# Other start addresses for split weights and matmul operands in a two-block transformer kernel

## The chip, the cores and the metric

The kernel runs on one core of one Trainium2 chip. The metric is the device time of one execution in microseconds (us). Before the change it is 894.39 us, the median of three runs (894.35 to 894.55).

## What is computed

Two transformer blocks over 256 tokens of width 1024, in float32. Nearly all the work is products of the activations with large weight matrices:

```python
# block one
proj = rms_norm(x) @ w_in                  # then block attention and gated linear attention
x = x + concat([y_moba, y_gla]) @ w_out
h = causal_dwconv(rms_norm(x) @ w_ffn_up)  # 1024 -> 2 * 2816
x = rms_norm(x + (silu(h_gate) * h_val) @ w_ffn_down)
# block two
x = x + 0.5 * g1 * swiglu(modulate(rmsnorm(x)), ffn1_w_in, ffn1_w_out)
z = modulate(rmsnorm(x)) @ w_in            # then latent attention and chunk attention
x = x + g2 * ((sigmoid(gate_a) * (o_a @ w_branch_a) + sigmoid(gate_b) * (o_b @ w_branch_b)) @ w_out)
x = rmsnorm(x + 0.5 * g3 * swiglu(modulate(rmsnorm(x)), ffn2_w_in, ffn2_w_out))
```

## The kernel before

Activations lie feature by token: 128 features in the partitions, 256 tokens (`S`) side by side, and the 1024 features of a row block as `KD = 8` tiles. A weight matrix is read as tiles of 128x128, and each is the stationary operand of a matmul with 256 (or 258) columns of activations moving past it.

To keep float32 precision at the fast matmul rate, each number is split into a high and a low half (`F32R`). A product then takes three matmuls: weight high x activation high, weight high x activation low, weight low x activation high. Where the two halves of an activation lie side by side in one tile (`Operand.beside`), the first two are one matmul of 512 columns, and the product is a pair: one of 512 columns and one of 256 (`lin_b`).

Weights come in chunks of up to 1024 columns, eight 128x128 tiles. `Stream` loads a chunk by a DMA on SyncE's queue into `wraw` (5 buffers), ScalarE copies it into `whi`, VectorE subtracts to get `wlo` (4 buffers each, used in turn). The order of all instructions on each engine is fixed when the program is built: a planner with a model of costs (`Clock`) decides when the side work of attention, norms and splits is slipped between the matmuls. That model knows nothing of addresses.

The stages, in order, with what the stream of weights meets in each:

| stage | moving operand | steps |
|---|---|---|
| attention input of block one (`mix1`) | `xhi`, `xlo`, 256 columns | 336 of 256 columns; 96 with the weights moving, 512 columns |
| `out1` | `yh`, `yl` | 192 of 256 columns |
| `up1` | `nh`, `nl` | 960 of 256 columns, after 64 plain float32 ones |
| `down1` | `hh` (high and low side by side) | 176 pairs of 512 and 256 columns |
| `ff1up` | raw `xhi`, `xlo` (258 columns), then `nh` | 240 of 258 columns, then 816 of 256 |
| `ff1down` | `hh` | 176 pairs |
| `mix2`, merge, `out2` | `xhi`/`xlo`, `nh`/`nl`, `qlh`/`qll` (latents), `oah`, `obh`, `mh` | 936 of 256 columns on `nh`, `oa`, `ob` and `mh`; others |
| `ff2up` | raw `xhi`, `xlo` (258 columns), then `nh` (side by side) | 240 of 258 columns, then 272 pairs |
| `ff2down` | `hh` | 176 pairs |

Each tile has an address in SBUF, the same in all 128 partitions. A tile starts where the one before it in its pool ended. In the built program all buffers of `whi` and `wlo` are 4096 bytes long and all start at 32 bytes modulo 512, and a 128-column slice is 512 bytes, so every weight tile starts at 32 modulo 512. So do `yh`, `yl`, `nh`, `nl`, `hh`, `oah`, `obh`, `mh` and `ml`, whose rows are 1024 or 2048 bytes. Others lie elsewhere: `xhi` at 192 and `xlo` at 256 modulo 512, and `qlh` and `qll` at 224. In the raw stages a row of `xhi` and `xlo` is 258 columns, 1032 bytes, so each step of the contraction starts 8 bytes further on.

The tiles that the change touches: `hi` and `lo` in `Stream.prep` (lines 240 and 241), `yo` (977), `ho` and `no` of the first feed-forward (1239 and 1240) and of `swiglu` (1390 and 1391), with `Operand.beside`. What follows are the functions that the diff touches and what calls them.

Of the kernel before, what the change touches and what calls it, by code (L numbers as in the profile page):

```python
# [11 lines left out]
F32R = mybir.dt.float32r  # L12
# [6 lines left out]
P = 128  # L19
D = 1024  # L20
S = 256
KD = D // P
FF = 2816
NF = FF // P
CH = 1024
# [69 lines left out]
def plan():  # L95
# [6 lines left out]
    def group(entries, width=CH, whole=False):  # L102
        first = len(chunks)
        cur, w = [], 0
        for e in entries:
            ew = sum(b - a for a, b in e[2])
            if w + ew > width:
                chunks.append(cur)
                cur, w = [], 0
            cur.append(e)  # L110
            w += ew
        if cur:
            chunks.append(cur)
        if whole:
            uncut.update(range(first, len(chunks)))

    def lin(name, c0, nk=KD, whole=False):
        group(tiles_t(name, [(c0, c0 + P)], nk), whole=whole)
# [25 lines left out]
    def ffn(up, down):  # L144
        for n in range(NF):
            lin(up, P * n, whole=up == "w_ffn_up" and n < RAW_PAIRS[up])
            lin(up, FF + P * n, whole=up == "w_ffn_up" and n < RAW_PAIRS[up])
        group([(down, k, [(P * n, P * n + P)]) for n in range(8) for k in range(NF)])
# [28 lines left out]


BESIDE = {"ffn2_w_in_2"}
RAW_PAIRS = {'w_ffn_up': 2, 'ffn1_w_in_2': 5, 'ffn2_w_in_2': 5}  # L180
PLAN, UNCUT = plan()
CW = [sum(b - a for e in c for a, b in e[2]) for c in PLAN]
# [26 lines left out]
class Stream:  # L209
# [20 lines left out]
    def prep(self, upto):  # L230
        while self.n_prep <= min(upto, len(PLAN) - 1):
            c = self.n_prep
            w = CW[c]
            self.load(c)
            raw = self.raw.pop(c)
            self.n_prep += 1
            if c in UNCUT:
                self.ready[c] = (raw, raw)
                continue
            hi = self.pool.tile([P, CH], F32R, name="whi", bufs=SPLIT_BUFS)  # L240
            lo = self.pool.tile([P, CH], F32R, name="wlo", bufs=SPLIT_BUFS)
            self.act.activation(hi[:, :w], raw[:, :w], AF.Copy)
            self.ready[c] = (hi, lo)
            self.owed[c] = (raw, self.clock.t["act"])
# [46 lines left out]
class Operand:  # L291
# [7 lines left out]
    @classmethod  # L299
    def beside(cls, t, n):  # L300

        o = cls(t[:, :, 0:S], t[:, :, S:2 * S], n)
        o.both = t
        return o


class Clock:
# [212 lines left out]
def mark(clock, gen, flag):  # L520
    yield from gen
    flag.append(clock.last)
# [18 lines left out]
SPLIT_BUFS = 4  # L541
# [3 lines left out]
def block_kernel(ctx: ExitStack, tc: tile.TileContext, xin, wst, adaw, cin, vec, cst_a, cst_b, cst_l, wgu, pos,  # L545
# [72 lines left out]
    def spl(op, k, src, scale=None, w=S):  # L618

        hi, lo = op.h[:, k, :w], op.l[:, k, :w]  # L620
        if scale is None:
            A.activation(hi, src, AF.Copy)
        else:
            A.activation(hi, src, AF.Copy, scale=scale)
        yield
        if scale is None:
            V.tensor_tensor(lo, src, hi.bitcast(F32), OP.subtract)
        else:
            V.scalar_tensor_tensor(lo, src, scale, hi.bitcast(F32), op0=OP.mult, op1=OP.subtract)
        op.done[k] = True  # L630
# [250 lines left out]
    ypool = yctx.enter_context(tc.tile_pool(name="y1", bufs=1))  # L881
# [16 lines left out]
    for h in range(4):  # L898
        k = slice(2 * h, 2 * h + 2)
# [74 lines left out]
    gq = one.tile([P, 2, S], F32, name="gq", tag="gqt")  # L974
    gk = one.tile([P, 2, S], F32, name="gk", tag="gkt")

    yo = Operand(ypool.tile([P, KD, S], F32R, name="yh"), ypool.tile([P, KD, S], F32R, name="yl"), KD)
    am = {}

    STAGES = [(hp, tt) for hp in range(2) for tt in range(2)]  # L980
# [197 lines left out]
    def table(name, *kinds):  # L1178

        while any(s[2] in kinds for s in side.live):  # L1180
            yield
        A.preload_act_table_set(name)
# [53 lines left out]
    fctx = ExitStack()  # L1236
    hpool = fctx.enter_context(tc.tile_pool(name="hid1", bufs=1))
    fp = fctx.enter_context(tc.tile_pool(name="ffn1p", bufs=2))
    ho = Operand.beside(hpool.tile([P, NF, 2 * S], F32R, name="hh"), NF)
    no = Operand(hpool.tile([P, KD, S], F32R, name="nh"), hpool.tile([P, KD, S], F32R, name="nl"), KD)  # L1240
    r_row = const.tile([P, S], F32, name="r_row")
    ring = [hpool.tile([P, S + 2], F32, name=f"u{i}") for i in range(4)]
    for u in ring:
# [45 lines left out]
    for n in range(NF):  # L1289
        op = xo if n < RAW_PAIRS["w_ffn_up"] else no  # L1290
        side.room("gate", 2)
# [3 lines left out]
        cu = fp.tile([P, S], F32, name="cu", bufs=3)  # L1295
        if n < RAW_PAIRS["w_ffn_up"]:
            pads = [ring[cnt % 4], ring[(cnt + 1) % 4]]
# [38 lines left out]
    def late(n):  # L1336
        while state["ga"] is None:
            yield
        yield from spl(xo, n, x[:, n, :], state["ga"][:, n:n + 1])
# [47 lines left out]

    def swiglu(name, up, down, norm, xo, r_row, r_norm, a, sh, emit, mid=None, late=None):
        with tc.tile_pool(name=name, bufs=1) as hpool, tc.tile_pool(name=name + "p", bufs=2) as fp:
            ho = Operand.beside(hpool.tile([P, NF, 2 * S], F32R, name="hh"), NF)  # L1390
            no = Operand.beside(hpool.tile([P, KD, 2 * S], F32R, name="nh"), KD)

            def chain():
                yield from norm()
                yield
                yield from normalised(no, x, a, r_norm, sh)

            def gate_raw(g, b, ps):
                while not state["norm"]:
                    yield  # L1400
                V.tensor_tensor(g, ps[:, :S], r_row, OP.mult)
                V.tensor_copy(b, ps[:, S:S + 1])
                yield
                A.activation(g, g, AF.Silu, bias=b)

            def whole(t, ps):

                A.activation(t, ps[:, S:], AF.Copy)
                yield
                V.tensor_tensor(t, ps[:, :S], t, OP.add)  # L1410

            def gate_norm(g, ps):
                if beside:
                    yield from whole(g, ps)
                    yield
                    A.activation(g, g, AF.Silu)
                else:
                    A.activation(g, ps[:, :S], AF.Silu)
                yield

            def value(n, u, g, ps, is_raw, flag):
                if is_raw:
                    while not state["norm"]:
                        yield
                    V.tensor_tensor(u, ps[:, :S], r_row, OP.mult)
                    yield
                    while not flag:
                        yield
                    V.scalar_tensor_tensor(u, u, ps[:, S:S + 1], g, op0=OP.add, op1=OP.mult)
                else:  # L1430
                    if beside:
                        yield from whole(u, ps)
                    while not flag:
                        yield
                    V.tensor_tensor(u, u if beside else ps[:, :S], g, OP.mult)
                yield
                yield from spl(ho, n, u)

            beside = up in BESIDE

            def product():
                return lin_b(up, no, KD) if beside else lin_t(up, no, S)

            by.phase(name + "up")
            state["norm"] = False
            side.add(chain(), "chain", True)
            if late is not None:
                side.add(late(), "late")
            for n in range(NF):
                side.room("gate", 2)  # L1450
                side.room("pair", 2)
                g = fp.tile([P, S], F32, name="g", bufs=3)
                u = fp.tile([P, S], F32, name="u", bufs=3)
                fl = []
                if n < RAW_PAIRS[up]:
                    b = fp.tile([P, 1], F32, name="b", bufs=3)
                    side.run(mark(clock, gate_raw(g, b, lin_t(up, xo, S + 2)), fl), "gate")
                    side.run(value(n, u, g, lin_t(up, xo, S + 2), True, fl), "pair")
                else:
                    side.run(mark(clock, gate_norm(g, product()), fl), "gate")  # L1460
                    side.run(value(n, u, g, product(), False, fl), "pair")
                if mid is not None and n == 12:
                    side.add(mid())
            side.add(table(LNEXP, "gate", "pair"))
            side.room("late", 1)
            by.phase(name + "down")
            for n in range(KD):
                ps = lin_b(down, ho, NF)
                side.room("after", 2)
                side.run(emit(n, ps), "after")  # L1470
            side.drain()
# [69 lines left out]
    ypool = yctx.enter_context(tc.tile_pool(name="y2", bufs=1))  # L1541
    oa = Operand(ypool.tile([P, 4, S], F32R, name="oah"), ypool.tile([P, 4, S], F32R, name="oal"), 4)
    ob = Operand(ypool.tile([P, 4, S], F32R, name="obh"), ypool.tile([P, 4, S], F32R, name="obl"), 4)
    no = Operand(ypool.tile([P, KD, S], F32R, name="nh"), ypool.tile([P, KD, S], F32R, name="nl"), KD)
# [3 lines left out]
    w = "w_in_2"  # L1548
# [320 lines left out]
```

## Time and profile before

| | us |
|---|---|
| median of three runs | 894.39 |
| the profiled execution, whole | 894.01 |
| its span, from the first to the last instruction | 892.2 |
| TensorE busy in the span | 876.4 |
| VectorE busy | 725.8 |
| ScalarE busy | 514.1 |

The span of a profiled execution is a little shorter than its time, since what lies before the first and after the last instruction isn't in it. TensorE (PE in the rows) runs matmuls that overlap: a 128x256 one is listed with some 0.28 us, though the next starts 0.12 us after it. So a busy share of TensorE says only that it never stands idle. How fast it goes is read from the spacing of starts in the timeline, or from the length of a stage over the number of its matmuls. PEld is the load of the stationary operand, which overlaps the matmul before it.

### The profile page before, as it was taken

Reading aid. Unit: us, or ns where it says so; the run is one execution under the profiler, and the core shown is the slowest. Engines: PE = TensorE matmul, PEld = TensorE weight load, DVE = VectorE, ACT = ScalarE, POOL = GpSimd, SP = SyncE. Lnnn points to the kernel's source line nnn. Section 1 sums busy time; section 2 is a strip of 40 time slices with the busy share of each in tenths; the row PEclk is TensorE's granted clock in tenths of the full one; section 3 lists DMA queues with packets and bytes.
Section 4 is the critical chain, followed back from the end, with each engine's and each line's share of the span. In section 5 each row is a group of like instructions: output and inputs, shape, how many; then the busy total and the mean of one; then the engine's idle time right before and its main releaser. Section 6 shows DMA issues by size and latency. Waiting matters only on the chain.

```text
span 892.2 us, 16627 instructions
## 1 busy us (share of the span) xinstructions
PE 876.4 (98%) x6490; PEld 809.1 (91%) x6490; DVE 725.8 (81%) x1347; ACT 514.1 (58%) x892; POOL 39.6 (4%) x78
## 2 busy tenths in 40 slices
PE   8999999999999999999999999999999999999996
PEld 6878898999998889999998888999999998888885
DVE  5869677899998889989888788788889998776663
ACT  5846666666665557444554457665546756666441
POOL 0000000000001000010010000000000000000000
PEclk9999999999999999999999999999999999999999
DMA  8533344777778785788887845777767676555541
GB/s 307 186 123 126 118 149 156 246 242 228 230 219 282 281 265 183 239 304 274 281 305 263 274 162 179 249 243 230 222 222 235 197 251 212 187 183 173 189 142 48
DMA packets 54126, 191.95 MB, mean 215 GB/s; under 512 B 6016, under 2 KB 6528, under 8 KB 54048
## 3 DMA queue, kind: packets, MB, share of 16 engines
q1 hardware_dynamic: 42768, 151.28, 51.8%
q0 software_dynamic: 10560, 38.41, 13.5%
q10 hardware_dynamic: 720, 1.21, 0.4%
q8 instruction: 51, 0.84, 0.4%
q14 instruction: 27, 0.22, 0.1%
HBM read 189.82 MB, written 1.05 MB: 214 GB/s over the span
## 4 chain that ended last, share of the span: by engine, by line
PE 95%; DVE 2%; ACT 1%; DMA 1%; issue 0%; SPq 0%; DVEq 0%
PE acc L447 89%; PE sca L447 3%; PE sct L447 2%; DMA wraw<-in_wst_dram 1%; PE ob L447 1%; DVE x L447 0%; ACT whi L447 0%; DVE wlo L447 0%; ACT sw L447 0%; DVE ad L447 0%; DVE kcat L447 0%; DVE m L447 0%; ACT rsqt L447 0%; SPq L447 0%; DVE f L447 0%
## 5 line engine op out<-in xcount | busy, mean ns | idle before, releaser
L447 DVE TENSOR_TENSOR wlo<-wraw,whi 128x1024 fp32r<-128x1024 f32 (+1 forms) x277 | 333.3, 1212 | 39.5 <-ACT whi L447 37.3
L447 PE MATMUL acc<-nh,whi 128*128 128x256 f32 (+1 forms) x1320 | 336.5, 308 | 0.0
L447 ACT ACTIVATE whi<-wraw 128x1024 fp32r<-128x1024 f32 (+1 forms) x277 | 285.2, 1042 | 25.5 <-PE acc L447 16.4
L447 PE MATMUL acc<-nh,wlo 128*128 128x256 f32 x1048 | 290.3, 282 | 0.0
L447 PEld LDWEIGHTS acc<-nh,whi 128*128 128x128 f32 x1320 | 230.3, 191 | 11.6 <-issue 2.2
L447 PEld LDWEIGHTS acc<-nh,wlo 128*128 128x128 f32 x1048 | 200.1, 191 | 3.1
L447 PE MATMUL acc<-hh,whi 128*128 128x512 f32 x528 | 184.9, 398 | 0.0
L447 PE MATMUL acc<-hh,wlo 128*128 128x256 f32 x528 | 144.5, 281 | 0.0
L447 PE MATMUL acc<-nl,whi 128*128 128x256 f32 x504 | 142.5, 283 | 0.0
L447 PEld LDWEIGHTS acc<-hh,whi 128*128 128x128 f32 x528 | 97.8, 188 | 22.1
L447 PEld LDWEIGHTS acc<-hh,wlo 128*128 128x128 f32 x528 | 99.7, 189 | 2.6 <-DVE wlo L447 0.3
L447 PEld LDWEIGHTS acc<-nl,whi 128*128 128x128 f32 x504 | 96.6, 192 | 0.1
L447 DVE SCALAR_TENSOR_TENSOR adraw<-adraw,crow 128x1024 f32<-128x1024 f32 x72 | 87.7, 1219 | 6.9 <-DMA adraw<-in_adaw_dram 6.9
L447 PE MATMUL acc<-xhi,whi 128*128 128x258 f32 (+2 forms) x312 | 90.9, 291 | 1.2 <-DVE x L447 1.2
L447 PE MATMUL acc<-xlo,whi 128*128 128x258 f32 (+2 forms) x312 | 88.1, 282 | 0.0
L447 PE MATMUL acc<-xhi,wlo 128*128 128x258 f32 (+2 forms) x312 | 87.7, 281 | 0.0
L447 POOL DMA_DIRECT2D adraw<-in_adaw_dram x72 | 38.2, 530 | 694.6 <-DVE adraw L447 418.6
L447 PEld LDWEIGHTS acc<-xhi,whi 128*128 128x128 f32 (+1 forms) x312 | 58.4, 187 | 3.7 <-issue 2.9
L447 PEld LDWEIGHTS acc<-xlo,whi 128*128 128x128 f32 (+1 forms) x312 | 58.5, 187 | 0.5
L447 PEld LDWEIGHTS acc<-xhi,wlo 128*128 128x128 f32 (+1 forms) x312 | 58.5, 188 | 0.0
L447 DVE SCALAR_TENSOR_TENSOR x<-acc,half_g,x 128x256 f32<-128x256 f32 x40 | 19.3, 483 | 24.8 <-PE acc L447 24.1
L447 ACT ACTIVATE hh<-u 128x256 fp32r<-128x256 f32 x44 | 18.4, 417 | 32.3 <-DVE u L447 32.3
(287 smaller groups left out, 1154.6 us busy)
## 6 DMA issues: line engine op xcount, KB each, us to landing
wraw<-in_wst_dram SPq DMA_DIRECT2D x277, 512.0 KB, 4.4
adraw<-in_adaw_dram POOLq DMA_DIRECT2D x72, 512.0 KB, 5.1
wraw<-in_wst_dram SPq DMA_DIRECT2D x7, 256.0 KB, 3.1
rb<-in_rel_dram SPq DMA_DIRECT2D x4, 384.0 KB, 4.3
f<-in_cst_l_dram SPq DMA_DIRECT2D x1, 576.0 KB, 6.6
x<-in_xin_dram SPq DMA_DIRECT2D x2, 256.0 KB, 6.1
x<-in_xin_dram ACTq DMA_DIRECT2D x2, 256.0 KB, 6.7
crow<-in_cin_dram POOLq DMA_DIRECT2D x1, 512.0 KB, 7.7
```

What stands on the lines that cost most here:

```text
L447: return f(*args, **kw)
```

## The change

The split weight buffers `whi` and `wlo` become 128 bytes longer (`STAGGER = 32` floats). With four buffers each, their starts are now 32, 160, 288 and 416 modulo 512, and high and low half of a chunk start at the same one. The operand tiles of six stages get some unused floats ahead of the first row (`SKIP`; `rows` cuts them off again). In `up1` the two halves `nh` and `nl`, two tiles before, become one with the halves side by side; the matmuls on them stay as they were, three of 256 columns. What is computed, the count of instructions, their order on each engine and their semaphores stay the same.

```diff
+STAGGER = 32
+SKIP = {"up1": 8, "ff1up": 8, "ff1down": 8, "ff2up": -8 % 128, "ff2down": 24, "out1": 24}
...
-            hi = self.pool.tile([P, CH], F32R, name="whi", bufs=SPLIT_BUFS)
-            lo = self.pool.tile([P, CH], F32R, name="wlo", bufs=SPLIT_BUFS)
+            hi = self.pool.tile([P, CH + STAGGER], F32R, name="whi", bufs=SPLIT_BUFS)
+            lo = self.pool.tile([P, CH + STAGGER], F32R, name="wlo", bufs=SPLIT_BUFS)
...
+def rows(pool, k, w, name, skip=0):
+
+    t = pool.tile([P, skip + k * w], F32R, name=name)
+    return t[:, skip:].rearrange("p (k w) -> p k w", k=k)
...
-    yo = Operand(ypool.tile([P, KD, S], F32R, name="yh"), ypool.tile([P, KD, S], F32R, name="yl"), KD)
+    yo = Operand(rows(ypool, KD, S, "yh", SKIP["out1"]), rows(ypool, KD, S, "yl"), KD)
...
-    ho = Operand.beside(hpool.tile([P, NF, 2 * S], F32R, name="hh"), NF)
-    no = Operand(hpool.tile([P, KD, S], F32R, name="nh"), hpool.tile([P, KD, S], F32R, name="nl"), KD)
+    ho = Operand.beside(rows(hpool, NF, 2 * S, "hh"), NF)
+    no = Operand.beside(rows(hpool, KD, 2 * S, "nh", SKIP["up1"]), KD)
...
-            ho = Operand.beside(hpool.tile([P, NF, 2 * S], F32R, name="hh"), NF)
-            no = Operand.beside(hpool.tile([P, KD, 2 * S], F32R, name="nh"), KD)
+            ho = Operand.beside(rows(hpool, NF, 2 * S, "hh", SKIP[name + "down"]), NF)
+            no = Operand.beside(rows(hpool, KD, 2 * S, "nh", SKIP[name + "up"]), KD)
```

Where an operand starts in the built programs, in bytes modulo 512 (the weights: 32 before; 32, 160, 288 and 416 in turn after):

| stage | before | after | after, distance from the weights modulo 128 |
|---|---|---|---|
| `out1` | 32 | 128 | 96 |
| `up1` | 32 | 64 | 32 |
| `down1` | 32 | 32 | 0 |
| `ff1up` | 32 | 96 | 64 |
| `ff1down` | 32 | 64 | 32 |
| `ff2up` | 32 | 96 | 64 |
| `ff2down` | 32 | 128 | 96 |
| `mix2` (`nh`, `oah`, `obh`), merge, `out2` | 32 | 32 | 0 |
| `mix1` and the raw stages | 192 and 256 | 192 and 256 | 32 and 96 (raw: and 8 more each step) |

## Rows read from the trace of the kernel before

**Rows 1.** The page: busy time (share) and instructions of each engine; the chain by line.

```profile
PE 876.4 (98%) x6490; PEld 809.1 (91%) x6490; DVE 725.8 (81%) x1347; ACT 514.1 (58%) x892; POOL 39.6 (4%) x78
...
PE acc L447 89%; PE sca L447 3%; PE sct L447 2%; DMA wraw<-in_wst_dram 1%; PE ob L447 1%; DVE x L447 0%; ACT whi L447 0%; DVE wlo L447 0%; ACT sw L447 0%; DVE ad L447 0%; DVE kcat L447 0%; DVE m L447 0%; ACT rsqt L447 0%; SPq L447 0%; DVE f L447 0%
```

**Rows 2.** Windows by stage: up1, down1, ff1up, ff1down, ff2up, ff2down; columns in the first row.

```profile
core 0: us, PE busy (x) PEld busy (x) DVE busy (x) ACT busy (x) POOL busy (x), PEclk, DMA share, GB/s
...
150.70:266.00 115.30, 115.30 (x962) 115.27 (x961) 108.10 (x183) 74.61 (x123) 5.29 (x10) 1.00 0.76 234
266.00:328.30 62.30, 62.27 (x354) 53.93 (x354) 53.66 (x88) 33.60 (x48) 5.83 (x11) 1.00 0.80 272
...
357.90:455.80 97.90, 97.90 (x818) 97.90 (x818) 84.81 (x136) 47.36 (x72) 9.54 (x18) 1.00 0.84 280
455.90:517.80 61.90, 61.90 (x354) 53.77 (x352) 51.26 (x79) 29.49 (x38) 5.83 (x11) 1.00 0.81 270
...
724.50:820.30 95.80, 95.80 (x546) 83.38 (x545) 73.49 (x112) 58.03 (x102) 1.06 (x2) 1.00 0.63 207
820.40:882.50 62.10, 62.10 (x353) 53.90 (x352) 33.06 (x43) 27.75 (x36) 0.00 (x0) 1.00 0.41 128
```

**Rows 3.** Timeline of TensorE in up1 (start us, us, engine, instruction): seven starts.

```profile
169.83 0.28 PE L447 MATMUL acc<-nh,wlo 128*128 128x256 f32 x1
...
170.55 0.28 PE L447 MATMUL acc<-nh,wlo 128*128 128x256 f32 x1
```

**Rows 4.** Timeline of TensorE in mix1: first and last of 43 starts in a row.

```profile
72.91 0.28 PE L447 MATMUL acc<-xlo,whi 128*128 128x256 f32 x1
...
77.88 0.28 PE L447 MATMUL acc<-xlo,whi 128*128 128x256 f32 x1
```

**Rows 5.** Timeline of TensorE on the latents: first, fifth and last of nine starts.

```profile
577.31 0.28 PE L447 MATMUL acc<-qll,whi 128*128 128x256 f32 x1
...
577.78 0.28 PE L447 MATMUL acc<-qlh,wlo 128*128 128x256 f32 x1
...
578.23 0.28 PE L447 MATMUL acc<-nh,whi 128*128 128x256 f32 x1
```

**Rows 6.** Timeline, raw stages: two runs of 209 starts, and three steps in the second.

```profile
333.10 0.28 PE L447 MATMUL acc<-xlo,whi 128*128 128x258 f32 x1
...
357.83 0.28 PE L447 MATMUL acc<-xhi,wlo 128*128 128x258 f32 x1
...
695.51 0.29 PE L447 MATMUL acc<-xhi,whi 128*128 128x258 f32 x1
...
695.89 0.28 PE L447 MATMUL acc<-xhi,whi 128*128 128x258 f32 x1
...
699.33 0.28 PE L447 MATMUL acc<-xlo,whi 128*128 128x258 f32 x1
...
724.42 0.28 PE L447 MATMUL acc<-xhi,wlo 128*128 128x258 f32 x1
```

**Rows 7.** Timeline, weights moving: 20 starts over `xhi`, 21 over `nh`, first and last.

```profile
92.87 0.39 PE L447 MATMUL acc<-whi,xlo 128*128 128x512 f32 x1
...
97.30 0.39 PE L447 MATMUL acc<-wlo,xhi 128*128 128x512 f32 x1
...
542.83 0.39 PE L447 MATMUL acc<-whi,nh 128*128 128x512 f32 x1
...
547.41 0.39 PE L447 MATMUL acc<-wlo,nh 128*128 128x512 f32 x1
```

**Rows 8.** Timeline of TensorE in down1: the first and the fourth pair's start.

```profile
285.08 0.39 PE L447 MATMUL acc<-hh,whi 128*128 128x512 f32 x1
...
286.12 0.39 PE L447 MATMUL acc<-hh,whi 128*128 128x512 f32 x1
```

**Rows 9.** Groups by form on VectorE: count, busy us, mean ns of one, idle before.

```profile
L447 DVE SCALAR_TENSOR_TENSOR xlo<-x,a,xhi 128x256 fp32r<-128x256 f32 x16 | 7.7, 481 | 2.3 <-ACT xhi L447 2.3
L447 DVE SCALAR_TENSOR_TENSOR nh<-nt,adav,nh 128x256 fp32r<-128x256 f32 x16 | 7.6, 478 | 0.0
```

## The prediction

> **What bounds the kernel now.** I read the page's busy shares and its chain first [rows 1]. TensorE is busy for 98% of the span, and 89% of the chain of waits that ends last is its matmuls into `acc`. [...] VectorE is the next busiest: 108.1 of 115.3 us in the up stage, 84.8 of 97.9 us in the first SwiGLU's up stage. So the time is a count of matmuls times the spacing of their starts. The profiled run took 894.01 us around a span of 892.2 us; the median of three is 894.39 us. I make the sum against 894.0 and add 0.4 at the end.
>
> The timeline of TensorE gives the spacing. In the up stage, where weights and operands all start at 32 modulo 512, six starts span 170.55 - 169.83 = 0.72 us, 120.0 ns each [rows 3]. In the attention's input stage, the operands start at 192 (high) and 256 (low), so 160 and 224 bytes past the weights, and 42 steps of the same 128x256 matmul take 77.88 - 72.91 = 4.97 us, 118.3 ns each [rows 4]. With the latent operands at 224 (192 past the weights), eight steps take 0.92 us, 115.0 ns each, the last four 112.5 ns [rows 5]. The clock, the shape and the engine are the same in all three. The bases differ. That is the evidence that this change touches what bounds the kernel.
>
> It is not evidence that a difference always helps. The raw stages read rows of 258 columns, so the base moves by 8 bytes with each step of the contraction. One of them takes 24.73 / 208 = 118.9 ns a step and the other 25.09 / 208 = 120.6 ns at equal bases, and three steps in the second take 0.38 us, about 126 ns each [rows 6]. And where 512 columns move, equal bases are the faster: 4.58 / 20 = 229.0 ns, against 4.43 / 19 = 233.2 ns where they differ [rows 7].
>
> **The change, part by part.** The two built programs hold the same 9,652 instructions, 6,114 of them matmuls, in the same order on each engine and with the same semaphores. Nothing is moved past a queue and no wait is added. Only addresses differ, so the sum has one kind of term: steps times a change of spacing. In the changed program the four buffers of high halves, and the four of low halves, start at 32, 160, 288 and 416 modulo 512, and successive chunks of weights go through them in turn. What stays fixed is the operand's distance from a weight modulo 128: 0 in down1, mix2, merge and out2; 32 in up1 and ff1down; 64 in ff1up and ff2up; 96 in out1 and ff2down.
>
> I take the nearest row for each distance, and assume that 128 bytes more or less changes nothing; that is a choice. Distance 64 is nearest to the latent operands (192 = 128 + 64): 115.0 ns, the whole run rather than its best end. Distances 32 and 96 are nearest to the attention's input stage (160 and 224): 118.3 ns. Distance 0 stays at 120.0.
> - up1: 960 steps, 120.0 to 118.3: 960 x 1.7 = 1.6 us.
> - ff1up: 816 steps, 120.0 to 115.0: 4.1 us.
> - out1: 192 steps, 120.0 to 118.3: 0.3 us.
> - Stages that alternate 512 and 256 columns have a pair as their step. Before, ff1down takes 61.9 / 176 = 351.7 ns a pair, ff2down 62.1 / 176 = 352.8, ff2up 95.8 / 272 = 352.2 [rows 2]. A run of three pairs with equal bases takes 1.04 us, 346.7 each [rows 8], so the pair has its own scatter. For the changed pair I add 231 ns (midway between 229.0 and 233.2, [rows 7]) to the 256-column value. ff2up: 231 + 115.0 = 346.0, 272 x 6.2 = 1.7 us. ff1down: 349.3, 176 x 2.4 = 0.4 us. ff2down: 176 x 3.5 = 0.6 us.
> - down1 (176 pairs), mix2, merge and out2 (936 steps): 0. If the step of 128 alone brought them to the 118.3 and 349.3 above, they would give 936 x 1.7 + 176 x 4.7 (from 62.3 / 176 = 354.0, [rows 2]) = 2.4 us more.
> - Raw stages (480 steps) and the attention's input (336): their distances modulo 128 stay as they were: 0. The two raw stages differ by 1.7 ns at equal distances, so the bound is 480 x 1.7 = 0.8 us on either side.
> - VectorE and ScalarE writing to shifted tiles: 0. A VectorE split pass takes 481 ns where its base walks in steps of 8 bytes and 478 where it stands still [rows 9].
>
> The sum is 1.6 + 4.1 + 0.3 + 1.7 + 0.4 + 0.6 = 8.7 us: 894.0 - 8.7 = 885.3, and with 0.4 for the median **885.7 us**. What hides the rest keeps up: ff1up would need 4.1 us from VectorE's slack of 97.9 - 84.8 = 13.1, and up1 1.6 us from 7.2.
>
> **Bounds.** At best, all 2,904 aligned 256-column steps go to 112.5 ns and all 800 pairs to 229.0 + 112.5 = 341.5: 2,904 x 7.5 + 800 x 11 = 30.6 us, a time of 864, which up1's VectorE would partly hold back (960 x 7.5 = 7.2 us is its whole slack). At worst, all steps go to the 126 of the slow triple, and pairs to 233.2 + 126 = 359: 2,904 x 6 + 800 x 6.5 = 22.6 us, a time of 917. Both ends ask one extreme of every base at once; stages that pass through four bases will mix them.
>
> [...] The timelines show the same matmul at 112.5, 115.0, 118.3, 120.0 and 126 ns under different bases [rows 3 to 6]. [...]
>
> **Rivals.**
> 1. *Addresses matter, but the four bases average out to what equal bases give.* Each chunk has another distance, and the time is an average over good and bad ones. For it: the second raw stage, with its eight bases, stands at 120.6, no better than 120.0. Against it: the other streams at unequal bases average below 120. It gives 894.4 (892.6 to 896.2). So would the case in which the weight read and the operand read never meet. Chance 0.15 for both. [...]
> 2. *Slower: losing the common start.* With equal bases the up stage holds its 120.0 ns [rows 3]. With stepping bases a stream could fall again and again into what the slow triple shows. The price: 256-column steps midway between 118.3 and 126, about 122, and pairs at 233.2 + 122 = 355.2, against 352.5: 2,904 x 2 + 800 x 2.7 = 8.0 us, so 902. It decides once the mean spacing of the 256-column steps is above 120.0. For it: 233.2 against 229.0 [rows 7], and the triple. Against it: the two streams of 256 columns at unequal bases stand at 118.3 and 115.0 [rows 4, 5]. Chance 0.12.
> 3. *Much more than I take:* the latent operands' last four steps (112.5 ns) hold for every shifted stage, and pairs go to 341.5. Shifted steps are 1,968 and shifted pairs 624: 1,968 x 7.5 + 624 x 10.7 = 21.4 us, a time of 873. For it: that run kept getting faster, so its whole mean includes a start. Against it: it is one short run, and only distance 64 is like it. Chance 0.15.
> 4. *Another engine becomes the bound.* In up1 VectorE leaves 7.2 us, so no gain there can exceed it. At my 1.6 us this changes nothing; it caps rival 3, and is counted there.
>
> **How the numbers follow.** My forecast has 0.58, with a range of its own from 877 to 892. The cases faster by over 0.2% (about 1.8 us, what a measurement of this kernel can tell from no change) are it and rival 3: 0.73. Same is rival 1: 0.15. Slower is rival 2: 0.12. The range for 8 in 10 runs from 872, which leaves out the far half of rival 3, to 897, which takes in all of rival 1 and leaves out most of rival 2.
>
> **What would show it.** The count of instructions and the waits by name stay; only the lengths of stages change. Right would be: ff1up about 93.8 us instead of 97.9 and starts some 115 ns apart; ff2up 94.1 instead of 95.8; up1 113.7 instead of 115.3; down1, mix2, merge and out2 as long as before. If down1 and mix2 shorten as well, the repeat is not 128 bytes and the step of the weight buffers works by itself. If ff1up stays at 120 ns, the latent row was not a case of the same thing. If spacing changes from chunk to chunk within a stage, the four buffers do differ. The prediction is wrong as a whole if the stages with shifted operands are no shorter than before, or if TensorE begins to wait for VectorE or for the weights.

## The result, and the profile after

The changed kernel takes 883.74 us, the median of four runs (883.64 to 884.27), against 894.37 (894.12 to 894.55) for the kernel before beside it: a ratio of 0.9883 [0.9865, 0.9900], 10.6 us faster. The prediction was 885.7 us.

The page of the changed kernel, its busy line and its chain by line, to be laid beside [rows 1]:

```profile
PE 865.6 (98%) x6490; PEld 800.1 (91%) x6490; DVE 724.4 (82%) x1347; ACT 514.1 (58%) x892; POOL 39.4 (4%) x78
...
PE acc L455 88%; PE sca L455 3%; PE sct L455 2%; PE ob L455 1%; DMA wraw<-in_wst_dram 1%; DVE wlo L455 1%; ACT whi L455 1%; DVE x L455 0%; ACT sw L455 0%; DVE ad L455 0%; DVE kcat L455 0%; DVE m L455 0%; ACT rsqt L455 0%; SPq L455 0%; DVE a
```

The counts of instructions are those of before. TensorE is still busy for 98% of the span and its matmuls into `acc` are 88% of the chain. What fell is TensorE's own busy time, 876.4 - 865.6 = 10.8 us: the same matmuls are started closer together.

The windows by stage after the change, in the order up1, down1, ff1up, ff1down, ff2up, answer to [rows 2]. (These windows run to the first matmul of the next stage; before, ff1down cut in that way is 63.38 us, since some work on the residual lies at its end.)

```profile
core 0: us, PE busy (x) PEld busy (x) DVE busy (x) ACT busy (x) POOL busy (x), PEclk, DMA share, GB/s
150.40:263.02 112.62, 112.62 (x963) 112.59 (x961) 107.58 (x183) 74.37 (x123) 5.27 (x10) 1.00 0.78 239
263.02:325.02 62.00, 61.91 (x354) 53.93 (x353) 53.93 (x88) 33.82 (x48) 5.81 (x11) 1.00 0.79 274
354.84:447.65 92.81, 92.81 (x819) 92.81 (x817) 83.93 (x136) 47.21 (x72) 9.51 (x18) 1.00 0.86 294
447.65:510.17 62.52, 61.33 (x355) 53.75 (x353) 52.42 (x82) 29.69 (x39) 5.80 (x11) 1.00 0.79 277
714.83:810.48 95.65, 95.65 (x546) 83.53 (x545) 73.54 (x112) 58.05 (x102) 1.06 (x2) 1.00 0.62 207
```

TensorE still has no idle time in up1 and ff1up, and the granted clock is 1.00 in every row, as before: neither a wait nor the clock has changed. up1 is 2.8 us shorter by first starts (115.39 to 112.62), ff1up 5.1. ff2up, which has operands at the same distance from the weights as ff1up, has hardly moved: 95.65 against 95.80.

The timeline of TensorE shows the spacing. First ff1up (start us, us, engine, instruction), near the stage's beginning and later:

```profile
360.03 0.28 PE L455 MATMUL acc<-nh,wlo 128*128 128x256 f32 x1
...
363.21 0.28 PE L455 MATMUL acc<-nh,wlo 128*128 128x256 f32 x1
...
389.73 0.28 PE L455 MATMUL acc<-nh,wlo 128*128 128x256 f32 x1
...
392.79 0.28 PE L455 MATMUL acc<-nh,wlo 128*128 128x256 f32 x1
```

Each pair of rows is 27 starts apart. The first 27 take 3.18 us, 117.8 ns each; the second 27 take 3.06 us, 113.3 ns each. Same instruction, same operand tile, same stage: ff1up has two spacings, and the experiments below come back to that.

Then the pairs of 512 and 256 columns, six pairs in ff1down (the first two rows) and five in ff2up:

```profile
470.93 0.39 PE L455 MATMUL acc<-hh,whi 128*128 128x512 f32 x1
...
473.01 0.39 PE L455 MATMUL acc<-hh,whi 128*128 128x512 f32 x1
...
760.20 0.39 PE L455 MATMUL acc<-nh,whi 128*128 128x512 f32 x1
...
761.96 0.40 PE L455 MATMUL acc<-nh,whi 128*128 128x512 f32 x1
```

In ff1down a pair takes 2.08 / 6 = 346.7 ns, in ff2up 1.76 / 5 = 352.0. The operand of ff1down is 32 bytes past the weights modulo 128, that of ff2up 64. A few pairs tell little, since three pairs at distance 0 also gave 346.7 [rows 8]; the lengths of the stages say the same: ff1down lost 0.87 us, 4.9 ns a pair, and ff2up 0.20 us, 0.7 ns a pair. For 256 columns alone 64 is the better of the two; for pairs it seems to be 32, and e5 below puts ff2up itself there.

### The profile page after: what moved, and what is told of

The parts are those of the page before. It is cut to its first block, busy times and chain, and to the rows that moved or that the text cites. A ratio compares the mean times of both kernels' runs of the same rounds, so it can differ in the third digit from the quotient of the medians.

```text
span 881.9 us, 16627 instructions
## 1 busy us (share of the span) xinstructions
PE 865.6 (98%) x6490; PEld 800.1 (91%) x6490; DVE 724.4 (82%) x1347; ACT 514.1 (58%) x892; POOL 39.4 (4%) x78
## 4 chain that ended last, share of the span: by engine, by line
PE 94%; DVE 2%; ACT 1%; DMA 1%; issue 1%; SPq 0%; DVEq 0%
PE acc L455 88%; PE sca L455 3%; PE sct L455 2%; PE ob L455 1%; DMA wraw<-in_wst_dram 1%; DVE wlo L455 1%; ACT whi L455 1%; DVE x L455 0%; ACT sw L455 0%; DVE ad L455 0%; DVE kcat L455 0%; DVE m L455 0%; ACT rsqt L455 0%; SPq L455 0%; DVE adraw L455 0%
## 5 line engine op out<-in xcount | busy, mean ns | idle before, releaser
L455 PE MATMUL acc<-nh,whi 128*128 128x256 f32 (+1 forms) x1640 | 353.0, 299 | 0.0
L455 PE MATMUL acc<-nh,wlo 128*128 128x256 f32 x1048 | 287.4, 280 | 0.0
L455 PEld LDWEIGHTS acc<-nh,whi 128*128 128x128 f32 x1640 | 263.5, 188 | 11.5 <-issue 2.2
L455 PEld LDWEIGHTS acc<-nh,wlo 128*128 128x128 f32 x1048 | 197.1, 188 | 2.9
L455 PE MATMUL acc<-nl,whi 128*128 128x256 f32 x184 | 51.8, 282 | 0.0
L455 PEld LDWEIGHTS acc<-nl,whi 128*128 128x128 f32 x184 | 34.9, 190 | 0.1
```

The lines of the kernel that those rows point to most:

```text
L455: return f(*args, **kw)
```

## The experiments

Three theories were set against one another first. **A**: the distance between the starts of moving operand and weights sets the spacing. **B**: the operand's own address does. **C**: the stepping of the weight buffers does the work, whatever the distance. For the later runs: **D**, at a distance of 64 modulo 128 a stream has two steady spacings, and stepping brings it into the faster; **E**, which spacing comes up is chance; **F**, addresses alone set it, so a kernel that is run again repeats it exactly.

The table has the length of each stage before, and what each kernel's profile adds or takes, in us. A stage runs from its first matmul's start to the first of the next stage; ff2down runs to the start of the last matmul of all. Merge counts with mix2, and out1 holds the 64 plain float32 matmuls ahead of up1.

| stage | before | after | e1 tiles only | e2 buffers only | e3 | e4 | e5 | e6 | e7 (e3) | e8 (e6) | e9 (e5) |
|---|---|---|---|---|---|---|---|---|---|---|---|
| out1 | 40.02 | -0.16 | +0.02 | -0.13 | -0.49 | -0.01 | -1.10 | -0.39 | -0.49 | -0.39 | -1.10 |
| up1 | 115.39 | -2.77 | -3.19 | -0.80 | -6.02 | -0.01 | -5.29 | -4.90 | -5.68 | -2.13 | -4.87 |
| down1 | 62.33 | -0.32 | -0.14 | -0.27 | +0.07 | -0.03 | -0.71 | -0.77 | +0.09 | -0.77 | -0.78 |
| ff1 raw | 29.55 | +0.27 | +0.01 | +0.27 | +0.34 | +0.35 | +0.29 | +0.34 | +0.35 | +0.01 | +0.29 |
| ff1up | 97.91 | -5.11 | -1.80 | -0.67 | -3.55 | 0 | -5.11 | -1.93 | -2.12 | -1.80 | -4.18 |
| ff1down | 63.38 | -0.87 | -0.87 | -0.36 | +0.09 | 0 | -0.86 | -0.87 | +0.10 | -0.87 | -0.87 |
| mix2 | 152.79 | -0.32 | -0.08 | -0.32 | -2.09 | +0.01 | -2.77 | -1.34 | -2.31 | -1.29 | -2.77 |
| out2 | 23.11 | -0.16 | 0 | -0.15 | -0.42 | -0.01 | -1.06 | -0.42 | -1.25 | -0.42 | -1.26 |
| ff2up | 95.85 | -0.20 | -0.52 | -0.21 | +0.02 | +0.03 | -1.45 | -0.89 | +0.02 | -0.89 | -1.45 |
| ff2down | 64.21 | -0.42 | -0.53 | -0.54 | -0.06 | 0 | -1.02 | -1.01 | -0.06 | -1.01 | -1.02 |

mix1 moves by less than 0.08 everywhere, the second raw stage by less than 0.17.

### Each half of the change alone (e1, e2)

e1 keeps the shifted tiles and takes the stepping of the buffers away; every weight tile is again at 32 modulo 512:

```diff
-STAGGER = 32
+STAGGER = 0
```

> The shifted operand tiles alone: weight buffers back to 4096 bytes, all starting at 32 modulo 512. Theory A (the spacing of matmuls goes by the operand's distance from the weight tile, repeating every 256 bytes): ff1up stays at distance 64 and about 113.9 ns a step (92.9 us, before 97.9); up1 at distance 32 about 116.5 ns (112 us, before 115.4); down1, mix2 and out2 back to 120.0 ns; 885 us in all. Theory B (the operand's own address sets it, the weights' doesn't matter): the same 885 us. Theory C (the stepping of the weight buffers does the work): back to 894 us.

e2 keeps the stepping and takes the shifts away:

```diff
-SKIP = {"up1": 8, "ff1up": 8, "ff1down": 8, "ff2up": -8 % 128, "ff2down": 24, "out1": 24}
+SKIP = {"up1": 0, "ff1up": 0, "ff1down": 0, "ff2up": 0, "ff2down": 0, "out1": 0}
```

> The longer weight buffers alone, all operand tiles back to 32 modulo 512. Theory A: steps alternate by chunk between 120.0 ns (distances 0 and 256) and some 118.5 ns (128 and 384): up1 114.7 us, ff1up 97.3 us, 892 us in all. Theory B: 894.4 us. Theory C: 884 us.

e1 took 886.92 us (885.31 to 887.56), a ratio of 0.9912 [0.9897, 0.9927]; e2 890.97 (890.49 to 891.91), 0.9962 [0.9948, 0.9976]. Against 894.42 beside them, the tiles bring 7.5 us and the buffers 3.4, about the 10.6 of both together. By stage they don't add. The windows of up1 and ff1up, here and below with the columns of the windows above, e1:

```profile
150.77:262.96 112.19, 112.19 (x962) 112.16 (x961) 106.88 (x183) 74.89 (x123) 5.26 (x10) 1.00 0.78 241
...
354.71:450.82 96.11, 96.11 (x818) 96.11 (x817) 84.36 (x136) 47.31 (x72) 9.50 (x18) 1.00 0.85 284
```

and e2:

```profile
150.41:264.99 114.58, 114.58 (x962) 114.55 (x961) 108.21 (x183) 74.51 (x123) 5.27 (x10) 1.00 0.75 235
...
356.86:454.10 97.24, 97.24 (x818) 97.24 (x817) 84.70 (x136) 47.32 (x72) 9.51 (x18) 1.00 0.84 284
```

In up1 the shift alone is better than the whole change (112.19 against 112.62 us). In ff1up the shift brings 1.8 and the stepping 0.7, and together they bring 5.1. Here theory A missed: it expected 92.9 us for ff1up in e1, and at its fixed distance of 64 the stage took 96.11 us, 117.8 ns a step from its first chunk to its last. Its figures for up1 in e1 and for both stages of e2 came out.

e2 also shows what stepping by itself is worth. Its 40 chunks of up1 read 120.0, 118.3, 120.0, 118.3 ns and so on, as the distance goes through 256, 384, 0 and 128 (means of the starts in a chunk, without the one break of 0.3 us at the start of the stage, matched with the addresses of the built program). So here the spacing repeats every 256 bytes, not every 128. In the changed kernel's up1 the chunks alternate as well: 116.6 ns at 32 and 288, 117.5 at 160 and 416. e1 stands at 32 alone, so the second kind of chunk is what stepping costs up1: 20 x 24 x 0.9 ns = 0.4 us. In out1 the changed kernel's chunks read 120.0 ns at 96 and 352, and 118.3 at 224 and 480; e1, at 96 alone, gains nothing there (+0.02 us).

### Distance or address (e3, e4)

Two kernels of before, with other tiles made longer so that what lies behind them in SBUF moves. e3 moves the weights by 64 bytes and leaves the operands where they were (operand at 32, weights at 96, a distance of 448):

```diff
-        t = work.tile([P, 512], F32, name="rsqt", bufs=1)
+        t = work.tile([P, 512 + 112], F32, name="rsqt", bufs=1)
...
-    half_g3 = const.tile([P, 8], F32, name="half_g3")
+    half_g3 = const.tile([P, 8 + 16], F32, name="half_g3")[:, :8]
```

> The kernel before with every weight buffer moved up by 64 bytes (to 96 modulo 512) and every operand tile left where it was (32). Theory A: the distance is 448, which is 192 modulo 256, the distance at which ff1up ran at 113.4 ns; so all 2904 steps of 256 columns go to 113.4 to 114 ns: up1 109.3 us, ff1up 92.9 us, mix2 and out2 some 5 us shorter together, 876 to 878 us in all. Theory B: no operand was moved, 894.4 us.

e4 moves weights and operands together:

```diff
-    half_g3 = const.tile([P, 8], F32, name="half_g3")
+    half_g3 = const.tile([P, 8 + 16], F32, name="half_g3")[:, :8]
```

> The kernel before with the weight buffers and all tiles allocated behind them moved up by 64 bytes together: operands and weights both at 96 modulo 512, distance 0. Theory A: 120.0 ns as before, 893 to 896 us (the attention input and the raw stages, whose operands stay, get other distances). Theory B: ff1up's operand starts at 96 as in the changed kernel and runs at 113.9 ns there, and so does up1: 880 to 884 us.

e3 took 882.95 us (879.28 to 884.03), 0.9863 [0.984, 0.9887]; e4 894.31 (893.99 to 896.08), 1.0 [0.9991, 1.0009]. The windows of up1 in e3 and ff1up in e3:

```profile
150.38:259.75 109.37, 109.29 (x963) 109.06 (x961) 105.38 (x183) 75.66 (x123) 5.27 (x10) 1.00 0.79 244
...
352.04:446.41 94.37, 92.79 (x819) 92.59 (x817) 83.17 (x135) 46.14 (x72) 9.50 (x18) 1.00 0.84 284
```

and in e4:

```profile
150.78:266.16 115.38, 115.38 (x963) 115.35 (x961) 108.54 (x183) 74.39 (x123) 5.27 (x10) 1.00 0.75 234
...
358.36:456.27 97.91, 97.91 (x818) 97.91 (x817) 85.05 (x136) 47.26 (x72) 9.50 (x18) 1.00 0.84 282
```

Moving both changes these stages by at most 0.01 us. Moving the weights alone, with the operands at their old address, takes 6.0 us off up1. Theory B falls and A stands: it is the distance. C falls as the only cause: e3 has no stepping at all and is as fast as the whole change. The size that A gave for e3, 876 to 878 us, was missed by some 5 us: most of out1 and all of out2 stood at 117.8 ns and not at 113.3, mix2 and out2 together gained 2.5 us where 5 were expected, and ff1up met a wait.

e3 shows a new wait too. ff1up in it has 1.58 us in which TensorE is not busy (94.37 - 92.79), though its steps are 113.3 ns apart. The waits in ff1up of e3 (engine, line, waited for: us in total, times, longest):

```profile
DVE adraw L447 <- DMA adraw<-in_adaw_dram: 5.0, 3, 4.3
...
PEld acc L447 <- DVE wlo L447: 1.8, 1, 1.8
PE acc L447 <- DVE wlo L447: 1.6, 1, 1.6
```

and VectorE's timeline there:

```profile
375.88 1.23 DVE L447 SCALAR_TENSOR_TENSOR adraw<-adraw,crow 128x1024 f32<-128x1024 f32 x1 [4.27 <-DMA adraw<-in_adaw_dram]
...
377.24 1.22 DVE L447 TENSOR_TENSOR wlo<-wraw,whi 128x1024 fp32r<-128x1024 f32 x1
```

A side pass on `adraw` stands ahead of the split of the next weights. It waits 4.27 us for its DMA and starts at 375.88; the split starts at 377.24, and TensorE then waits 1.6 us for `wlo`. VectorE is not full there (83.17 of 94.37 us); it is held. This is the mechanism of rival 4 in another form: a faster stream meets a queue whose order was planned for a slower one.

### A version made from this (e5), and the same without stepping (e6)

e5 puts the stages of 256 columns (out1, up1, ff1up, mix2, merge, out2) at 64 modulo 128 from the weights, and all stages of pairs at 32; `oah` and the `hh` of down1 get a shift as well. The raw stages and mix1 keep their distances, and the few steps on the latents go from 64 to 0. e6 is e5 without the stepping:

```diff
-SKIP = {"up1": 8, "ff1up": 8, "ff1down": 8, "ff2up": -8 % 128, "ff2down": 24, "out1": 24}
+SKIP = {"up1": 8, "ff1up": 8, "ff1down": 8, "ff2up": 0, "ff2down": 8, "out1": 16, "down1": 8, "mix2": 16}
...
-    ho = Operand.beside(rows(hpool, NF, 2 * S, "hh"), NF)
+    ho = Operand.beside(rows(hpool, NF, 2 * S, "hh", SKIP["down1"]), NF)
...
-    oa = Operand(ypool.tile([P, 4, S], F32R, name="oah"), ypool.tile([P, 4, S], F32R, name="oal"), 4)
+    oa = Operand(rows(ypool, 4, S, "oah", SKIP["mix2"]), ypool.tile([P, 4, S], F32R, name="oal"), 4)
```

> The changed kernel with other shifts, weight buffers stepping as in the change: every stage of 256-column steps (out1, up1, ff1up, mix2, merge, out2) at 64 modulo 128 from the weights, every stage of pairs (down1, ff1down, ff2up, ff2down) at 32. Theory D (two steady spacings at distance 64, about 113.4 and 117.8 ns; stepping the buffers restarts the stream at each chunk and lets it fall into the faster): up1 109.5 us, ff1up 92.8 us as in the changed kernel, mix2 149 us, out2 22 us, pairs at 347.6 ns (ff2up 94.5, the down stages 0.9 us shorter each than in the kernel before), 873 to 876 us in all. Theory E (ff1up's 113.4 ns in the changed kernel was luck of its start, stepping does nothing for it): some of these stages at 117.8 ns, 879 to 883 us.

e6, beside that:

```diff
-STAGGER = 32
+STAGGER = 0
```

> The same shifts, but weight buffers of 4096 bytes, so that each stage keeps one distance: 64 for the 256-column steps, 32 for the pairs. Theory D: a stage stays in whichever of the two spacings it starts in; ff1up at 117.8 ns again (96.1 us), up1 either 109 or 113 us, runs scatter by some us, 878 to 884 us. Theory E: no difference to the stepping one beyond luck; both scatter alike.

e5 took **875.44 us** (874.77 to 875.75), 0.9783 [0.9768, 0.9797]: 19.1 us less than before, and 8.3 less than the change as it was made. e6 took 883.08 (881.3 to 884.68), 0.9874 [0.9853, 0.9895]. Both medians lie in the ranges that theory D gave, and e5 lies below the 879 to 883 us of theory E. So with these distances the stepping is worth 7.6 us, though alone (e2) it was worth 3.4. The windows of e5, of up1, down1, ff1up and ff2up:

```profile
149.58:259.68 110.10, 109.59 (x963) 109.37 (x961) 105.49 (x183) 75.66 (x123) 5.26 (x10) 1.00 0.77 243
259.68:321.29 61.61, 61.42 (x354) 53.83 (x353) 53.89 (x88) 33.62 (x48) 5.80 (x11) 1.00 0.81 278
351.13:443.94 92.81, 92.81 (x819) 92.81 (x817) 83.74 (x135) 47.06 (x72) 9.51 (x18) 1.00 0.87 289
707.78:802.18 94.40, 94.40 (x546) 83.18 (x545) 73.55 (x112) 57.99 (x102) 1.05 (x2) 1.00 0.63 210
```

ff2up at distance 32 is 94.40 us, 1.25 less than at 64: 347.1 ns a pair (94.40 / 272) against 351.7. Both have stepping buffers. Without stepping the two distances lie closer together: 95.33 us at 64 (e1, first row) and 94.96 at 32 (e6), 350.5 and 349.1 ns a pair. So for pairs too the step of the buffers has a part, and why is open.

```profile
718.54:813.87 95.33, 95.33 (x546) 83.28 (x545) 73.53 (x112) 57.96 (x102) 1.05 (x2) 1.00 0.63 208
...
714.03:808.99 94.96, 94.96 (x547) 83.25 (x545) 73.54 (x112) 58.01 (x102) 1.06 (x2) 1.00 0.63 208
```

up1 at 64 is 2.5 us less than at 32.

### Once more, to tell chance from address (e7, e8, e9)

e3, e6 and e5 as they were, one profile each.

> The same program as the one with weights moved up by 64 bytes, profiled a second time. Theory D (two steady spacings for one set of addresses, entered by the state in which a stream starts): some stage takes another length than in the first profile, by 113.4 against 117.8 ns a step (up1 109.4 or some 113 us, ff1up about 92.6 or 96 us). Theory F (addresses alone set the spacing): each stage as in the first profile to 0.1 us: up1 109.4, out1 39.5, out2 22.7 us.

> The same program as the one with shifts 64 and 32 and no stepping, profiled a second time. Theory D: up1 and ff1up split otherwise between 113.4 and 117.8 ns than in the first profile (110.5 and 96.0 us). Theory F: 110.5 and 96.0 us again.

> The same program as the one with shifts 64 and 32 and stepping buffers, profiled a second time. Theory D: stepping restarts the stream at each chunk, so the stages repeat: up1 110.1, ff1up 92.8 us to 0.3 us. If stepping doesn't hold the stream in the faster spacing, they move by some us as in the kernel without it.

They took 882.4, 884.3 and 875.69 us. F falls: the same program with the same addresses does not always run at the same spacing. e9 repeats e5 in whole time, but not to the 0.3 us a stage that D had expected: up1 took 110.52 us against 110.10, ff1up 93.73 against 92.81. The window of up1 in e6:

```profile
150.12:260.60 110.48, 110.22 (x962) 109.99 (x961) 105.57 (x183) 75.69 (x123) 5.27 (x10) 1.00 0.79 240
```

and in e8, the same program:

```profile
150.24:263.50 113.26, 113.26 (x963) 113.24 (x962) 107.84 (x183) 74.50 (x123) 5.27 (x10) 1.00 0.78 238
```

In e8 all 40 chunks of up1 stand at 117.7 to 117.8 ns (the break at the start of the stage left out). In e6 the first nine stand there, the tenth holds a wait, and the other thirty stand at 113.3. In e7, ff1up begins with nine chunks at 113.3 and ends with 24 at 117.8; in e3 it stays at 113.3 throughout. These are two steady spacings at one set of addresses.

**What moves a stream from one to the other.** D had expected a stage without stepping to stay in whichever spacing it starts in, and that was too simple. Without stepping I found a change within up1, ff1up and out2, at 64 modulo 128, at three places only (up1 and ff1up of e6, ff1up of e7), and each time TensorE had just waited. The waits around the second of them, in e6:

```profile
DVE adraw L455 <- DMA adraw<-in_adaw_dram: 3.3, 1, 3.3
PEld acc L455 <- DVE wlo L455: 0.8, 1, 0.8
PE acc L455 <- DVE wlo L455: 0.6, 1, 0.6
```

and TensorE's timeline ahead of that wait and behind it:

```profile
375.74 0.28 PE L455 MATMUL acc<-nh,wlo 128*128 128x256 f32 x1
...
376.42 0.28 PE L455 MATMUL acc<-nh,wlo 128*128 128x256 f32 x1
...
377.96 0.28 PE L455 MATMUL acc<-nh,wlo 128*128 128x256 f32 x1
...
380.79 0.28 PE L455 MATMUL acc<-nh,wlo 128*128 128x256 f32 x1
```

Ahead of it six starts take 0.68 us, 113.3 ns each; behind it 24 take 2.83 us, 117.9 each, and it stays so to the end of the stage. A wait can also leave the spacing as it was (ff1up of e3, after its 1.6 us), and it can help (up1 of e6, after 0.3 us). It stayed fast in up1 of e7 too, after 0.4 us. Where no wait came (ff1up of e1, both stages of e8), nothing changed for the whole stage. It need not be a wait: in out1 of e3 and e7 starts go from 113 to 118 ns apart where four `ob` matmuls of another shape stand between two steps. What the changes have in common is a break in the stream.

With stepping, each slow stretch of an uninterrupted stream ended, and always at the same step. The weight buffers are used from the highest address down, and one step in four goes back up, from the lowest to the highest; there the distance goes from 64 to 192. In the changed kernel's ff1up the chunks read 117.8, 117.9, 117.7 ns at distances 320, 448 and 64, and then 113.3 from the chunk at 192 on, for all the 31 that are left. In ff1up of the changed kernel, and in up1, ff1up and out2 of e5 and e9, a slow stretch met that step eight times, and left it eight times at 113.3 to 113.6. Two of these stretches, in e9, had begun at a wait of TensorE (0.7 us in up1, 0.5 in ff1up), and the next wrap ended them. So D stands, with one addition: it is not every chunk's step that does it, but the wrap. E holds for fixed buffers, and with stepping only for whether a slow stretch begins at a wait (up1 of e5 stayed fast after one of 0.5 us).

Not tried: a wait put in on purpose at a fixed place, which would show that the wait itself decides. That every change without stepping comes at a break of the stream has been seen at these few places, and not more. Nor is it settled why the wrap works and the step from 320 to 448, the same modulo 256, does not.

## Why the prediction was right, and where it was not

The time came out 2.0 us below the forecast, well inside its range. The main mechanism of the forecast held: only the spacing of starts changed, and the distance of operand and weights changes it. But some of that agreement is luck: ff2up brought 1.5 us less than its term, while up1, ff1up, ff1down and the stages put at nothing brought 3.5 more. And the part of the stepping in ff1up was not foreseen. By stage, predicted and measured (profile against profile):

| term | predicted | measured | |
|---|---|---|---|
| up1 | -1.6 | -2.77 | too small |
| ff1up | -4.1 | -5.11 | too small |
| ff2up | -1.7 | -0.20 | **wrong** |
| ff1down | -0.4 | -0.87 | too small |
| ff2down | -0.6 | -0.42 | near |
| out1 | -0.3 | -0.16 | half |
| down1, mix2 with merge, out2 | 0 | -0.80 | the 128-byte assumption |
| raw stages and mix1 | 0 (0.8 either way) | +0.10 | within |
| sum | -8.7 | -10.2 | |

- **ff2up is the step that failed.** I took a pair as the sum of a 512-column row and a latent row, 231 + 115.0 = 346.0 ns, and found 352. The terms do not add like this: at distance 64 the stage gives 95.65 / 272 = 351.7 for the pair, and at 32 in e5 347.1, though single matmuls of 256 columns prefer 64. [Rows 7] are of another kind of product (the weights moving), and the row that was the right kind, [rows 8], had no second distance beside it. An honest bound for the pair was "not known, either sign", not a midpoint.
- **The repeat of 128 bytes was wrong, and cost little.** The prediction said what would show it: down1 and mix2 shortening as well. They do, by 0.32 us each, and e2 shows the reason: 118.3 ns at 128 and 384, 120.0 at 0 and 256. The sentence "if the step of 128 alone brought them to the 118.3" was right for every second chunk; the price that I put on it, 2.4 us, was three times what came (0.80).
- **up1 was sized from the far row.** For distance 32 I took [rows 4], at 160 and 224. Measured are 116.6 ns (32, 288) and 117.5 (160, 416) for single chunks. The chunk that had a matching distance, 160, is the one nearer to the row. out1, sized from the same row, came out at half, because its chunks at 96 and 352 stayed at 120.0.
- **ff1up was sized from a run that was still settling, and its gain put down to the distance alone.** [Rows 5] start at 117.5 (the first four steps) and end at 112.5 a step; I took the mean, 115.0. The steady value is 113.3, with three chunks at 117.8 ahead of it, together 113.7. But e1, at the same distance and without the stepping, gained 1.8 us of the 5.1 and stayed at 117.8 throughout. What brought the stream to 113.3 in the changed kernel was the wrap of the stepping buffers, for which the prediction had no term. Rival 3 said that the run's mean holds a start, and in that it was right for ff1up. It was wrong for the sum, because the pairs did not follow, and up1 at distance 32 stayed at 116.6 to 117.5.
- **Rival 1** (the buffers average out) is seen in up1, where stepping takes back 0.4 us of 3.2, but the average of its distances is 117.1 ns, below 120.0. **Rival 2** (losing the common start) is seen nowhere as a loss against before: with the stepping, no uninterrupted stream of 256 columns stood above the 120.0 it had. (The slow triple that prices it is 0.38 / 3 = 126.7 ns, not 126.) The first raw stage is 0.27 us longer, which is all there is on that side, and it need not be the stepping: it is +0.35 in e4, which has none, and +0.34 and +0.01 in e6 and e8, which are one program.
- **Rival 4** did not happen in the changed kernel: the windows have no idle TensorE in up1 and ff1up. It appears as soon as up1 goes to 113.3 (e3, e5, e9): its window then holds 0.1 to 0.7 us of idle TensorE. Where the waits were read, VectorE was not full but held by a DMA.

Rival 1 has a second case, in which the weight read and the operand read never meet; e4 against e3 decides it. The same weights, moved by the same 64 bytes, bring nothing (e4, -0.01 us) or 6.0 us (e3) in up1 according to where the moving operand lies. In that case e3 would have been as long as before, and e3 took 882.95 us against 894.42. Why the distance matters, and how the two are read, is not shown by any run here.

## What to carry to other kernels

Where TensorE is busy for 98% and never waits, look at the spacing of starts, stage by stage, before you call the kernel finished: here 5% of a stage lay in where its tiles start (up1 in e3: 6.0 of 115.4 us). Find the good distance between the start of the moving operand and that of the weights by moving one tile and measuring, for each shape of step separately (alone, or in pairs with a wider one), and don't carry it from one shape to another. A stream can have more than one steady spacing at the same addresses (up1 of one program: 113.3 ns in thirty chunks of e6, 117.7 to 117.8 in all forty of e8); here the wrap of buffers whose starts step brought it back into the fast one eight times out of eight, and one profile of a kernel without them can be luck.

## What was not expected of the hardware

- The spacing of 128x256 matmuls with a new weight tile each depends on the distance of the two operands' starts modulo 256: about 120.0 ns at 0 and at 96, 118.3 at 128 and at 224, 116.6 at 32, 117.5 at 160, and 113.3 at 64 and at 192 when settled. Nothing in the waits or in the busy shares tells of it: in ff1up TensorE is busy for the whole window at 120.0, at 117.8 and at 113.7 ns a step (before, e1, the changed kernel).
- At 64 modulo 128 there are two steady spacings, 113.3 and 117.8 ns, for the same program and the same addresses (e6 and e8). For up1 that is 960 x 4.5 ns = 4.3 us, and for ff1up 816 x 4.5 = 3.7 us. The runs of e6, 881.3 and 881.61 against 884.56 and 884.68, differ by about such an amount; only the profiled ones show their spacing.
- Pairs of 512 and 256 columns rank the distances otherwise: in ff2up 351.7 ns at 64 and 347.1 at 32 with stepping buffers, 350.5 and 349.1 without. At a fixed distance of 448 (e3), where single steps are the fastest of all, ff2up is as long as before (+0.02 us).
